# Two blocks of small experts moved to the third and last place, an earlier split of the first token tile, and a gating step moved into the last combination

## The chip, the cores and the metric

The kernel runs on one core of a Trainium2 chip. The metric is device time of one execution in microseconds (us); lower is better. A core has five engines with instruction streams of their own: TensorE (PE: matmuls and transposes; PEld is its weight load), VectorE (DVE), ScalarE (ACT), GpSimd (POOL) and SyncE (SP), which here issues the DMA transfers. They meet through semaphores.

## What is computed

Two layers over x of 512 tokens and 1024 channels, in f32:

```python
h = rms_norm(x, norm_mix)                  # all RMS norms over the 1024 channels
x = x + mixer(h)                           # dilated attention and conformer convolution, gated, w_out
h2 = rms_norm(x, norm_ffn)
# top-1 of 4 groups, then top-2 of 8 experts in it: 2 of 32 experts for each token
x = x + sum_e gate_e * (silu(h2 @ w_gate[e]) * (h2 @ w_up[e])) @ w_down[e]     # FF = 512
x = x + sigmoid(rms_norm(x, norm_ple) @ w_ple_gate) * (p @ w_ple_proj)
```

and a last RMS norm behind the second layer. Every token picks its own experts, so which experts have few tokens is known only at run time.

## The kernel before, in words

**Tiles.** x lies in 4 tiles of 128 tokens by 1024 channels. Dense weights (`wd`) come as chunks of 128 by 1024 (512 KB), are loaded raw (`s_raw`), scaled for the gating chunks (L234), and split into a high part (`s_hi`, ScalarE, L235) and a low part (`s_lo`, GpSimd L240, or in halves on GpSimd and VectorE). `mm3` (L311) multiplies such pairs with three matmuls, high by high, low by high and high by low; these are the rows of L313 to L315. `token_b` (L350) is 24 of these matmuls for one token tile over four chunks and 512 output columns; `tokens_b` runs it for the 4 tiles.

**Start.** `run` (L436) loads the x tiles and the first chunks in turn. For each tile it computes 1/rms (squares on ScalarE, a chain of tiny VectorE operations), then `prep` (L430) makes the normalised `s_n` on VectorE and appends to `todo` the transposes (`ps_tr`, L420) with their high and low halves `s_hTh` and `s_hTl`. An entry of `todo` is run when something pops it. The recording of this part (line 103 in the profile, where a helper records every operation) goes through a scheduler that places the instructions on each engine. Then comes `mixer` (L492). Its first step is the value projection: `tokens_b` over the chunks v0 to v3, into `ps_tb`; behind it the step with `ps_z` begins. `ahead` says how many chunks are split before they are needed.

**Mixture of experts.** `order_experts` (L935) counts the tokens of each expert and sorts: the first 4 experts are static, of the rest the 8 with the fewest tokens are the small ones. Each expert has a place in a table of slots: 64 for an ordinary one, 32 for a small one; tokens beyond that go through `overflow` (L1289), a loop with a count that is read at run time. A block has 128 slots: two ordinary experts (a pair) or four small ones (a quad). `BLK` lists the 14 blocks of a layer: 2 static pairs, 2 quads, 10 pairs. The weights of an expert are 12 tiles of 512 KB (four each of `wg`, `wu`, `wdn`), in a ring of slots that SyncE fills in the order in which they are used (L253).

The loop of `moe` (L1036) takes two blocks a turn, c = 0 to 6: gate and up of both (`ps_g`, `ps_u`), `hidden` (tanh and two products), down of the two blocks of the turn before (`ps_y`), transposes, the gather for the next turn (`ps_xg`), and the combination of the turn before into x (`ps_c`, L1144, `s_x` added at L1153). The experts of a block write to different rows of one PSUM tile, 64 rows each for a pair and 32 for a quad; TensorE runs these column groups side by side. In turn 2 stands the overflow, in turns 4 and 5 the embeddings' projection (`ps_pe`).

**Tail of a layer.** After the loop come the downs of blocks 12 and 13 and their combination, with a hook `then(t)` after each token tile: transposes of x (`ps_tr`, L1269), the parts `s_gTh` and `s_gTl`, the splits of the gating chunks pg0 to pg7 (a list says how many after which tile), and `first(t - 1)`, the first half of the gating matmuls (`ps_tb`). After all four, 1/rms of each tile (`rh`) is computed. `ple` (L1406) then does `gated(t, 0)` for the four tiles (tanh, product L1417, addition to x L1419), and `tokens_b` over pg4 to pg7 with `gated(t, 1)`, which ends with `prep` for the next layer or the last norm and the output.

## Time and profile before

| | |
|---|---|
| median of 3 runs | 1854.9 us (1853.12 to 1855.19) |
| the profiled execution | 1849.56 us, span 1847.8 us |
| mean granted clock of TensorE in it | 0.987 |
| busy: TensorE, VectorE, ScalarE, GpSimd | 95%, 47%, 29%, 21% of the span |
| chain that ended last | TensorE 62%, DMA 21%, VectorE 8%, issue 5% |
| moved by DMA | 478.66 MB, mean 259 GB/s |

The chain is followed back from the last instruction, at each step to what released it. A wait at one place of it belongs to one stage; the shares of the whole span do not say which stage has which limit. Matmuls overlap, so the step from one to the next is shorter than the duration of one (0.23 us against 0.39 us for 512 columns).

### The profile page before, as it was taken

To read this page: it belongs to the slowest core of one execution; us is meant where nothing else is said; L and a number is where in the kernel's file an instruction comes from. 1 tells how busy PE (TensorE), PEld (TensorE's weight loads), DVE (VectorE), ACT (ScalarE), POOL (GpSimd) and SP (SyncE) were. 2 spreads that over 40 slices of the span, in tenths; PEclk is the share of its full clock that TensorE was granted. 3 is DMA by queue.
4 is the path that set the end of the run, shared out by engine and by line. 5 is a ranking of instruction groups with operands and counts; after the bars stand their busy time and mean duration, and the time that the engine had idled before them with its cause. 6 is when DMAs were issued, how large, how long until landed. Compare 5 with 4: busy or idle time off the path is not lost.

```text
span 1847.8 us, 24216 instructions
## 1 busy us (share of the span) xinstructions
PE 1750.0 (95%) x8324; PEld 1055.2 (57%) x8324; DVE 871.8 (47%) x2131; ACT 544.6 (29%) x1041; POOL 379.6 (21%) x203
## 2 busy tenths in 40 slices
PE   5999999989889999999999999999989899999997
PEld 4776777753143455454877777777432443455356
DVE  5587864374041343223558777535620331443146
ACT  4355443321011012112634545342110110121045
POOL 3445332410200001000444443242002000010021
PEclk9999999999999999999999999999999999999999
DMA  5212126479999999997241112554899899999941
GB/s 224 84 65 68 58 79 232 145 264 384 419 359 404 419 419 419 416 419 300 86 133 58 60 57 69 180 195 139 307 391 419 341 418 419 419 414 419 419 197 46
DMA packets 133616, 478.66 MB, mean 259 GB/s; under 512 B 14832, under 2 KB 15344, under 8 KB 133488
## 3 DMA queue, kind: packets, MB, share of 16 engines
q1 hardware_dynamic: 133488, 477.06, 66.4%
q8 instruction: 68, 1.11, 0.2%
q14 instruction: 60, 0.49, 0.1%
HBM read 474.90 MB, written 2.10 MB: 258 GB/s over the span
## 4 chain that ended last, share of the span: by engine, by line
PE 62%; DMA 21%; DVE 8%; issue 5%; ACT 2%; POOL 1%; SPq 0%; POOLq 0%; DVEq 0%; ACTq 0%
DMA s_w<-wdn 11%; PE ps_g L103 8%; PE ps_xg L103 6%; PE ps_u L103 6%; PE ps_z L314 5%; PE ps_z L313 5%; PE ps_z L315 5%; PE ps_y L103 5%; DMA s_w<-wu 5%; PE ps_c L103 5%; DMA s_w<-wg 3%; PE ps_tb L313 2%; PE ps_tb L314 2%; PE ps_tb L315 2%; PE ps_S L634 2%
## 5 line engine op out<-in xcount | busy, mean ns | idle before, releaser
L240 POOL TENSOR_TENSOR s_lo<-s_raw,s_hi 128x1024 fp32r<-128x1024 f32 x114 | 274.8, 2422 | 838.2 <-ACT s_hi L235 464.5
L103 PE MATMUL ps_u<-s_w,s_xg 128*64 128x512 f32 (+1 forms) x1024 | 239.0, 595 | 12.2 <-DMA s_w<-wu 11.8
L103 PE MATMUL ps_g<-s_w,s_xg 128*64 128x512 f32 (+1 forms) x1024 | 225.0, 606 | 14.3 <-DMA s_w<-wdn 9.4
L103 PE MATMUL ps_y<-s_w,s_hT 128*64 128x512 f32 (+1 forms) x1024 | 222.9, 601 | 10.7 <-DMA s_w<-wdn 10.4
L314 PE MATMUL ps_z<-s_hTl,s_hi 128*128 128x512 f32 x512 | 203.9, 398 | 0.0
L313 PE MATMUL ps_z<-s_hTh,s_hi 128*128 128x512 f32 x512 | 201.4, 393 | 0.0
L315 PE MATMUL ps_z<-s_hTh,s_lo 128*128 128x512 f32 x512 | 199.8, 390 | 0.0
L103 PEld LDWEIGHTS ps_u<-s_w,s_xg 128*64 128x64 f32 (+1 forms) x1024 | 67.6, 130 | 178.0 <-issue 118.0
L103 PEld LDWEIGHTS ps_y<-s_w,s_hT 128*64 128x64 f32 (+1 forms) x1024 | 69.2, 131 | 161.7 <-issue 114.3
L103 PEld LDWEIGHTS ps_g<-s_w,s_xg 128*64 128x64 f32 (+1 forms) x1024 | 65.1, 132 | 162.0 <-issue 129.0
L526 DVE SCALAR_TENSOR_TENSOR s_acc<-ps_z,smt,s_acc 128x511 f32<-128x511 f32 (+27 forms) x210 | 153.7, 732 | 4.2
L235 ACT ACTIVATE s_hi<-s_raw 128x1024 fp32r<-128x1024 f32 x120 | 125.4, 1056 | 8.8 <-PE ps_wo L314 4.0
L1108 DVE SCALAR_TENSOR_TENSOR s_h<-s_h,ps_g 128x512 f32<-128x512 f32 x28 | 19.2, 687 | 212.0 <-ACT s_h L1107 194.5
L1107 ACT ACTIVATE s_h<-ps_g,rs 128x512 f32<-128x512 f32 x28 | 19.2, 687 | 328.9 <-PE ps_g L103 327.4
L1153 DVE TENSOR_TENSOR s_x<-s_x,ps_c 128x512 f32<-128x512 f32 x112 | 75.2, 685 | 77.1 <-PE ps_c L103 46.1
L314 PEld LDWEIGHTS ps_z<-s_hTl,s_hi 128*128 128x128 f32 x512 | 96.3, 188 | 21.4 <-issue 3.0
L313 PEld LDWEIGHTS ps_z<-s_hTh,s_hi 128*128 128x128 f32 x512 | 96.1, 188 | 21.3 <-issue 1.0
L103 PE MATMUL ps_xg<-s_OH,s_xh 128*128 128x256 f32 x412 | 104.3, 293 | 3.7 <-DVE s_lgT L944 3.7
L315 PEld LDWEIGHTS ps_z<-s_hTh,s_lo 128*128 128x128 f32 x512 | 96.3, 188 | 19.0
L1118 ACT ACTIVATE s_hT<-ps_hT 128x512 f32<-128x512 f32 x28 | 15.4, 596 | 298.8 <-PE ps_hT L103 298.8
L103 PE MATMUL ps_xg<-s_OH,s_xl 128*128 128x256 f32 x412 | 103.1, 290 | 0.0
L1109 DVE TENSOR_TENSOR s_h<-s_h,ps_u 128x512 f32<-128x512 f32 x28 | 19.2, 687 | 155.2 <-PE ps_u L103 155.2
(274 smaller groups left out, 2815.4 us busy)
## 6 DMA issues: line engine op xcount, KB each, us to landing
s_w<-wu SPq DMA_DIRECT2D x256, 512.0 KB, 9.9
s_w<-wdn SPq DMA_DIRECT2D x256, 512.0 KB, 9.9
s_w<-wg SPq DMA_DIRECT2D x248, 512.0 KB, 9.9
s_raw<-wd SPq DMA_DIRECT2D x124, 512.0 KB, 3.3
s_w<-wg SPq DMA_DIRECT2D x16, 256.0 KB, 7.6
s_x<-x SPq DMA_DIRECT2D x4, 512.0 KB, 9.7
out<-s_n SPq DMA_DIRECT2D x8, 256.0 KB, 2.0
s_gain<-gains SPq DMA_DIRECT2D x3, 512.0 KB, 5.1
```

What stands on the lines that cost most here:

```text
L103: i = f(*a, **k)
L235: nc.scalar.activation(hi, raw, AF.Copy)
L240: nc.gpsimd.tensor_tensor(lo, raw, hi.bitcast(F32), op=OP.subtract)
L313: mm(out, lh, rh, start=start, stop=False)
L314: mm(out, lh, rl, start=False, stop=False)
L315: mm(out, ll, rh, start=False, stop=stop)
L526: v.scalar_tensor_tensor(o, i, w, o, op0=OP.mult, op1=OP.add)
L634: nc.tensor.matmul(ps[:, off:off + n], qk(0, i * P, (i + 1) * P)[r], qk(1, 0, n)[r], start=True, stop=True)
L1107: act.activation(t, pg, AF.Tanh, scale=rh[p])
L1108: v.scalar_tensor_tensor(t, t, 1.0, pg, op0=OP.add, op1=OP.mult)
L1109: v.tensor_mul(t, t, pu)
L1153: v.tensor_add(xs, xs, ps)
```

## The change

It has three parts.

- **Blocks.** The two quads stood third and fourth; now they stand third and last, with the ten pairs between them. `order_experts` gets another rule for the slots' base.
- **Start.** In `run` the transposes of token tile 0 are popped right behind its own `prep`, and the splits of the value chunks are recorded as 0, then 1 and 2, then 3. The other tiles' transposes are popped in the middle of the value projection's `token_b` by a hook, in layer 0 alone. In that stage `ahead` is 1 instead of 4.
- **Gating.** 1/rms of a tile is computed in the combination's hook, and `first(t)` does `gated(t, 0)` at once. `gated` becomes a method; the body is the same.

```diff
--- before.py
+++ after.py
@@ -28,12 +28,12 @@
 GS = 256
 
 
+
 NST, NSM = 4, 8
 NDY = NE - NST
 LD = 4
-BLK = ([(2 * i, 2 * i + 1) for i in range(NST // 2)]
-       + [tuple(range(NST + 4 * i, NST + 4 * i + 4)) for i in range(NSM // 4)]
-       + [(i, i + 1) for i in range(NST + NSM, NE, 2)])
+BLK = ([(2 * i, 2 * i + 1) for i in range(NST // 2)] + [tuple(range(NST, NST + 4))]
+       + [(i, i + 1) for i in range(NST + NSM, NE, 2)] + [tuple(range(NST + 4, NST + NSM))])
 NB = len(BLK)
 
 
@@ -362,11 +362,11 @@
                 self.done(c)
         return ps
 
-    def tokens_b(self, cs, src, then):
+    def tokens_b(self, cs, src, then, hook=None):
         for c in cs:
             self.take(c)
         for t in range(NT):
-            then(t, self.token_b(cs, src, t))
+            then(t, self.token_b(cs, src, t, hook))
 
 
     def rsqrt(self, y, a, t, steps=3):
@@ -443,7 +443,9 @@
         for t in range(NT):
             if t:
                 nc.sync.dma_start(self.x[t], self.dr["x"][t * P:(t + 1) * P])
-            self.load_chunks(t)
+            if t < 3:
+                self.load_chunks(t)
+        self.load_chunks(3)
         self.small(0)
         self.load_chunks(5)
         self.load_c2()
@@ -456,9 +458,9 @@
         for t in range(NT):
             n = self.s4.get(F32, "n")
             self.prep(t, gain, self.rms(t, n), n)
-            if t in (1, 2):
+            self.split_chunks((0, 2, 3, 3)[t])
+            if t == 0:
                 self.todo.pop(0)()
-            self.split_chunks(t)
         self.nc = nc
         self.s4.free()
         for l in range(self.L):
@@ -493,7 +495,7 @@
         nc = self.nc
         v, act = nc.vector, nc.scalar
         base = l * NCH
-        self.look, self.ahead = LK[0], AH
+        self.look, self.ahead = LK[0], AH if l else 1
         pos = self.pos = {s: base + i for i, s in enumerate(SEQ_CHUNKS)}
         self.lim = pos["wo7"]
         conv, attn, side = [], [], []
@@ -505,10 +507,17 @@
         def value(t, ps):
             act.activation(vt(t), ps, AF.Copy)
             self.ps.free()
-            if self.todo:
+            if l and self.todo:
                 self.todo.pop(0)()
-        self.tokens_b([pos[f"v{i}"] for i in range(4)], self.hT, value)
-
+        halves = []
+
+        def middle():
+            halves.append(0)
+            if not l and len(halves) % KD == KD // 2 and self.todo:
+                self.todo.pop(0)()
+        self.tokens_b([pos[f"v{i}"] for i in range(4)], self.hT, value, middle)
+
+        self.ahead = AH
         if l:
             self.load_c2()
         self.scale_small(l)
@@ -937,6 +946,7 @@
         v = self.nc.vector
         cnt = self.posb[:, 128:160]
         key, rank, small, base, self.cnt, top, rest, bs = (self.lgT[:, 32 * i:32 * i + 32] for i in range(8))
+        bs32 = rest
         bs, ss = bs[:, :8], bs[:, 8:16]
         over = lambda a, n: a.unsqueeze(1).to_broadcast([P, n, 32])
         down = lambda a, n: a.unsqueeze(2).to_broadcast([P, n, 32])
@@ -958,10 +968,12 @@
         v.tensor_reduce(rank, t3, axis=AX.X, op=OP.add)
 
         v.tensor_scalar(small, rank, float(NSM), 32.0, op0=OP.is_lt, op1=OP.mult)
-        v.scalar_tensor_tensor(base, rank, float(NSM - 1), small, op0=OP.subtract, op1=OP.mult)
+
+        v.tensor_scalar(bs32, rank, 4.0, -40.0, op0=OP.is_ge, op1=OP.mult)
+        v.scalar_tensor_tensor(bs32, bs32, -11.0, rank, op0=OP.add, op1=OP.add)
+        v.tensor_mul(base, bs32, small)
         v.scalar_tensor_tensor(base, rank, float(CAP), base, op0=OP.mult, op1=OP.subtract)
-        if CAP * NST != CAP // 2 * NSM:
-            v.tensor_scalar(base, base, float(CAP * NST - CAP // 2 * NSM), None, op0=OP.add)
+        v.tensor_scalar(base, base, -128.0, None, op0=OP.add)
         v.tensor_copy(base[:, :NST], self.cc(C_BASE, NST))
         v.tensor_add(self.cnt, cnt, small)
         self.ps.free()
@@ -1254,10 +1266,8 @@
         self.rh = []
         self.src = [lambda k, a, b, s=s: s[a // P][:, k * P:(k + 1) * P] for s in gT]
         cs = [self.pos[f"pg{i}"] for i in range(4)]
-        self.pg = []
-
         def first(t):
-            self.pg.append(self.token_b(cs, self.src, t))
+            self.gated(t, 0, self.token_b(cs, self.src, t))
 
         def then(t):
             if t == NT - 1:
@@ -1273,17 +1283,16 @@
             split_after(PGS[t + 1])
             self.gT[0].append(hi)
             self.gT[1].append(lo)
+            junk = self.s2.get(F32, "j")
+            r = self.rms(t, junk)
+            self.s2.free()
+            h_ = self.tn(1, f"rh{t}")
+            v.tensor_scalar(h_, r, 0.5, None, op0=OP.mult)
+            self.rh.append(h_)
             if t:
                 first(t - 1)
         combine((NB - 2, NB - 1), then)
         first(NT - 1)
-        for t in range(NT):
-            junk = self.s4.get(F32, "j")
-            r = self.rms(t, junk)
-            self.s4.free()
-            h_ = self.tn(1, f"rh{t}")
-            v.tensor_scalar(h_, r, 0.5, None, op0=OP.mult)
-            self.rh.append(h_)
 
 
     def overflow(self, l):
@@ -1403,6 +1412,16 @@
             self.s4.used, self.s2.used, self.ps.used = was
 
 
+    def gated(self, t, h, ps):
+        nc = self.nc
+        th = self.s2.get(F32, "th")
+        self.last = nc.scalar.activation(th, ps, AF.Tanh, scale=self.rh[t]).ins
+        self.ps.free()
+        nc.vector.scalar_tensor_tensor(th, th, 1.0, self.pp[h](t), op0=OP.add, op1=OP.mult)
+        xs = self.x[t][:, h * T:(h + 1) * T]
+        self.last_v = nc.vector.tensor_add(xs, xs, th).ins
+        self.s2.free()
+
     def ple(self, l):
         nc = self.nc
         v, act = nc.vector, nc.scalar
@@ -1410,17 +1429,7 @@
         self.look, self.ahead = 3, 1
         last = l == self.L - 1
 
-        def gated(t, h, ps):
-            th = self.s2.get(F32, "th")
-            self.last = act.activation(th, ps, AF.Tanh, scale=self.rh[t]).ins
-            self.ps.free()
-            v.scalar_tensor_tensor(th, th, 1.0, self.pp[h](t), op0=OP.add, op1=OP.mult)
-            xs = self.x[t][:, h * T:(h + 1) * T]
-            self.last_v = v.tensor_add(xs, xs, th).ins
-            self.s2.free()
-
-        for t in range(NT):
-            gated(t, 0, self.pg[t])
+        gated = self.gated
         self.pp[0].free()
         gain = self.gain_row(l + 1)
         if not last:
```

The order of instructions, at three places. TensorE's first rows: `ps_tr` are transposes of a normalised token tile (`s_n_108` is tile 0, `s_n_131` and `s_n_149` tile 1), `ps_tb` the value matmuls of tile 0. Before:

```order
L420 MATMUL ps_tr_149<-c_71,s_n_108 128x128 x4
L420 MATMUL ps_tr_158<-c_71,s_n_108 128x128 x4
L420 MATMUL ps_tr_190<-c_71,s_n_131 128x128 x4
L420 MATMUL ps_tr_199<-c_71,s_n_131 128x128 x4
L313 MATMUL ps_tb_260<-s_hi_126,s_hTh_100 128x512
```

After:

```order
L420 MATMUL ps_tr_131<-c_71,s_n_108 128x128 x4
L420 MATMUL ps_tr_140<-c_71,s_n_108 128x128 x4
L313 MATMUL ps_tb_230<-s_hi_126,s_hTh_100 128x512
L314 MATMUL ps_tb_230<-s_lo_127,s_hTh_100 128x512
L315 MATMUL ps_tb_230<-s_hi_126,s_hTl_104 128x512
L313 MATMUL ps_tb_230<-s_hi_126,s_hTh_100 128x512
L314 MATMUL ps_tb_230<-s_lo_127,s_hTh_100 128x512
L315 MATMUL ps_tb_230<-s_hi_126,s_hTl_104 128x512
L313 MATMUL ps_tb_230<-s_hi_167,s_hTh_101 128x512
L314 MATMUL ps_tb_230<-s_lo_168,s_hTh_101 128x512
L315 MATMUL ps_tb_230<-s_hi_167,s_hTl_105 128x512
L313 MATMUL ps_tb_230<-s_hi_167,s_hTh_101 128x512
```

The transposes of tile 1 went from the second place to behind ten value matmuls of tile 0.

TensorE, a little further: `s_lo_196` is the low part of the last value chunk, `ps_tb_230` belongs to tile 0, `ps_tb_274` to tile 1, `s_n_177` is tile 2. After:

```order
L313 MATMUL ps_tb_274<-s_hi_167,s_hTh_101 128x512
L314 MATMUL ps_tb_230<-s_lo_196,s_hTh_103 128x512
L315 MATMUL ps_tb_230<-s_hi_195,s_hTl_107 128x512
L314 MATMUL ps_tb_274<-s_lo_168,s_hTh_101 128x512
L315 MATMUL ps_tb_274<-s_hi_167,s_hTl_105 128x512
L420 MATMUL ps_tr_287<-c_71,s_n_177 128x128 x4
```

The last two matmuls of tile 0 were set behind ten of tile 1.

VectorE in the last combination of layer 0, at its last token tile: `ps_c` is the combination's output, `s_gTl` the low part of the transposed x. Before:

```order
L1153 TENSOR_TENSOR s_x_3972<-s_x_3972,ps_c_6756 128x512
L1153 TENSOR_TENSOR s_x_3972<-s_x_3972,ps_c_6762 128x512
L1271 TENSOR_TENSOR s_gTl_6769<-ps_tr_6770,s_gTh_6768 128x512
L1271 TENSOR_TENSOR s_gTl_6769<-ps_tr_6777,s_gTh_6768 128x512
L393 TENSOR_SCALAR rms_6851<-ss_0_6847 128x1
```

After:

```order
L1165 TENSOR_TENSOR s_x_3902<-s_x_3902,ps_c_6824 128x512
L401 TENSOR_SCALAR rms_6781<-rms_6781 128x1
L1420 SCALAR_TENSOR_TENSOR s_th_6820<-s_th_6820,s_pp_5678 128x512
L402 TENSOR_SCALAR rms_6781<-rms_6781 128x1
L1422 TENSOR_TENSOR s_x_3900<-s_x_3900,s_th_6820 128x512
L1290 TENSOR_SCALAR rh_6793<-rms_6781 128x1
L1165 TENSOR_TENSOR s_x_3902<-s_x_3902,ps_c_6830 128x512
L1281 TENSOR_TENSOR s_gTl_6837<-ps_tr_6838,s_gTh_6836 128x512
```

Between the two additions of the last tile now stand steps of the 1/rms of tile 2, and the product (L1420) and addition (L1422) of tile 1's gating.

## Rows read from the trace of the kernel before

**Rows 1.** The page's slices of the span (40 equal slices of 46.2 us; busy tenths of TensorE, and what the DMA engines moved).

```profile
PE   5999999989889999999999999999989899999997
...
GB/s 224 84 65 68 58 79 232 145 264 384 419 359 404 419 419 419 416 419 300 86 133 58 60 57 69 180 195 139 307 391 419 341 418 419 419 414 419 419 197 46
```

**Rows 2.** SyncE's queue in time, and the page's list of DMA issues. Columns of the first four: start us, us from the first to the last issue, queue and line, what is loaded, how many tiles. The last row: size of one, median us from issue to landing.

```profile
798.00 9.08 SPq L253 DMA_DIRECT2D s_w<-wu  x8
...
808.00 39.58 SPq L253 DMA_DIRECT2D s_w<-wdn  x32
...
848.45 9.06 SPq L217 DMA_DIRECT2D s_raw<-wd  x8
...
1719.63 39.63 SPq L253 DMA_DIRECT2D s_w<-wdn  x32
...
s_w<-wdn SPq DMA_DIRECT2D x256, 512.0 KB, 9.9
```

**Rows 3.** The chain of waits, in order of time: start us, us, what (engine, tile written, line, how many). Layer 0 but for the last row, which is layer 1.

```profile
504.32 13.88 PE ps_y L103 x64
...
801.37 7.02 PE ps_g L103 x32
...
816.76 10.44 DMA s_w<-wdn
...
847.17 8.48 PE ps_c L103 x29
...
855.64 13.94 PE ps_y L103 x64
...
1765.03 13.93 PE ps_y L103 x64
```

**Rows 4.** TensorE's timeline in the first block of small experts (start us, us, line, tiles, matmuls in a row, in brackets the idle time before and what ended it), then a window: us, busy us (instructions) of PE, PEld, DVE, ACT, POOL, granted clock, DMA share, GB/s.

```profile
436.74 7.07 PE L103 MATMUL ps_g<-s_w,s_xg 128*32 128x512 f32 x64
...
446.82 2.25 PE L103 MATMUL ps_u<-s_w,s_xg 128*32 128x512 f32 x12 [1.29 <-DMA s_w<-wu]
...
452.49 2.26 PE L103 MATMUL ps_u<-s_w,s_xg 128*32 128x512 f32 x12 [0.18 <-DMA s_w<-wu]
...
450.00:475.00 25.00, 21.64 (x81) 3.90 (x80) 0.69 (x1) 0.00 (x0) 0.00 (x0) 1.00 1.03 419
```

**Rows 5.** A row of SyncE's queue, two windows (columns as above) and one row of TensorE's waits from 385 to 870 (line waited for: us in total, times, longest).

```profile
523.67 13.40 SPq L253 DMA_DIRECT2D s_w<-wu  x8
...
550.00:552.00 2.00, 0.00 (x0) 0.00 (x0) 0.00 (x0) 0.00 (x0) 0.00 (x0) 0.72 0.21 82
...
552.00:556.00 4.00, 3.20 (x8) 1.01 (x10) 0.06 (x1) 0.00 (x0) 0.00 (x0) 0.50 0.49 131
...
PE ps_g L103 <- DMA s_w<-wdn: 4.7, 1, 4.7
```

**Rows 6.** The timeline of the start on VectorE, TensorE and GpSimd, in order of time, and one window (columns as above).

```profile
15.34 2.13 DVE L103 SCALAR_TENSOR_TENSOR s_n<-s_x,rms,s_gain 128x1024 f32<-128x1024 f32 x1
...
17.62 1.94 PE L420 MATMUL ps_tr<-c,s_n 128*128 128x128 f32 x8 [5.26 <-DVE s_n L103]
...
19.21 0.78 PE L313 MATMUL ps_tb<-s_hi,s_hTh 128*128 128x512 f32 x1
...
19.82 2.02 DVE L103 TENSOR_SCALAR rms<-rms 128x1 int32<-128x1 int32 x9
...
20.64 0.63 PE L313 MATMUL ps_tb<-s_hi,s_hTh 128*128 128x512 f32 x1
...
21.07 0.63 PE L314 MATMUL ps_tb<-s_lo,s_hTh 128*128 128x512 f32 x1
...
26.23 8.04 POOL L240 TENSOR_TENSOR s_lo<-s_raw,s_hi 128x1024 fp32r<-128x1024 f32 x3 [1.34 <-ACT s_hi L235]
...
29.29 2.77 DVE L103 SCALAR_TENSOR_TENSOR s_n<-s_x,rms,s_gain 128x1024 f32<-128x1024 f32 x1
...
31.99 2.83 DVE L103 TENSOR_TENSOR s_lo<-s_raw,s_hi 128x512 fp32r<-128x512 f32 x1
...
34.87 0.50 PE L314 MATMUL ps_tb<-s_lo,s_hTh 128*128 128x512 f32 x1 [2.25 <-DVE s_lo L103]
...
37.00:39.00 2.00, 2.00 (x8) 1.71 (x7) 1.30 (x4) 1.81 (x5) 0.00 (x0) 0.52 0.28 109
...
48.85 0.39 PE L315 MATMUL ps_tb<-s_hi,s_hTl 128*128 128x512 f32 x1
...
49.08 0.39 PE L313 MATMUL ps_z<-s_hTh,s_hi 128*128 128x512 f32 x1
```

**Rows 7.** The end of layer 0: TensorE's waits from 862 to 1000, then the timeline of VectorE and GpSimd, then the matmuls of `ps_z` from 900 to 1000 (duration ns min/median/max, first and last start).

```profile
PE ps_tr L1269 <- DVE s_x L1153: 3.0, 3, 2.5
...
PE ps_tr L420 <- DVE s_n L432: 2.5, 2, 2.2
...
908.63 0.68 DVE L1417 SCALAR_TENSOR_TENSOR s_th<-s_th,s_pp 128x512 f32<-128x512 f32 x1
...
912.69 2.83 DVE L1417 SCALAR_TENSOR_TENSOR s_th<-s_th,s_pp 128x512 f32<-128x512 f32 x1
...
912.41 2.56 POOL L240 TENSOR_TENSOR s_lo<-s_raw,s_hi 128x1024 fp32r<-128x1024 f32 x1 [6.46 <-ACT s_hi L235]
...
L313 PE MATMUL ps_z<-s_hTh,s_hi x55: 387/389/397, 959.4 to 999.5; 128*128 128x512 f32 x55
```

## The prediction, made before the change was run

> **What bounds the kernel now.** I read the slices of the span first [rows 1]. TensorE's row is full except in the first slice, and the transfer row reaches its ceiling of 419 GB/s in two long stretches only, the two mixtures of experts (MoE). So the mixers are bound by TensorE, and inside the MoE two engines of about equal load share the lead: a pair of experts is 24 weight tiles, a quad of small ones 48, at 1.25 us a tile (eight tiles are issued in 9.08 us, seven steps [rows 2]), thus 30 and 60 us of transfer. TensorE needs the same time for either, because the column groups of a block run at once: 7.0 us for the 32 matmuls of a pair's gate group, 7.1 us for the 64 of a quad's [rows 3, 4]. A pair is balanced between the two, a quad is bound by its transfer.
>
> The chain of waits then says what ends each MoE [rows 3]. In layer 0 it runs over transfers from 816.76 on (10.44 us is the first of three such pieces), then a combination, and then 13.94 us of `ps_y` matmuls to 869.6 without a wait for a transfer. The last weight tile was issued at 808.00 + 39.58 = 847.6 and landed 9.9 us later, at 857.5 [rows 2]. TensorE thus ends 12.1 us behind the last byte. In layer 1 the same sum is 1719.63 + 39.63 + 9.9 = 1769.2 against 1765.03 + 13.93 = 1779.0, 9.8 us. This is the work of a pair that TensorE still has in hand when its transfer has ended.
>
> **Order of the blocks.** The bytes and their number stay. What moves is the transfer-bound block: 24 tiles (30 us) go from the fourth place to the last. TensorE, which reaches the downs of blocks 0 and 1 at 504.3 in layer 0 [rows 3], would no longer wait for a second quad before them, so it is about 20 us early there and, with the 8 down tiles less that follow, 30 us early after the next downs; the stream's order shifts by the same 24 tiles, and the pairs between see the same relation of slots and consumers. In the last two blocks the stream gets its 24 tiles back, while TensorE needs no more time, so it falls back to the transfer: down of blocks 10 and 11 is fed while landing, their combination and down of block 12 lie beside the last 24 tiles (30 us, against 8.48 us for 29 of 32 matmuls and half of 13.94), and down of block 13 eats its tiles as they land. After the last byte is left one quarter of a down (four steps over FF), 6.97/4 = 1.7 us. End of the MoE: 857.5 + 1.7 = 859.2 instead of 869.6, **−10.4 us** in layer 0, and 1770.9 instead of 1779.0, **−8.1 us** in layer 1. I count −10 and −8. The eight gating chunks are queued behind the last weights [rows 2]; 1.25 us apart they land from 858.8, and the first two are all that the next step on ScalarE asks for.
>
> The bounds: nothing at all, if the stream is held up by 10 us more than before, and −12 with −10 if the stream even closes one of its gaps. It has such gaps [rows 5]: where the up-weights of a block wait for slots (13.40 us for eight tiles instead of 9.08, 4.3 us) and around the overflow loop (82 GB/s from 550 to 552, while TensorE stood 4.7 us). Both stand at the same turn of the loop after the change, some 20 to 30 us earlier, and their instructions and slots are the same; I take them as unchanged.
>
> The longer rule for the slots' base is three more operations over 32 columns on VectorE, in a chain whose like last 0.22 us each (2.02 us for nine [rows 6]). They stand before the first transfer of a chosen expert, with the static blocks' tiles still in the queue as cover; I count nothing, and +1 per layer without that cover.
>
> **Start.** The PE rows of the start [rows 6] show the transposes of token tile 0 done at 12.36, idle 5.26 us until the normalised tile 1 (VectorE, 15.34 + 2.13), the first value matmul at 19.21, a stall before 34.87 (its last 2.25 us behind the low half of a split; that and `s_n` of tile 3 take 2.83 and 2.77 us on VectorE beside three GpSimd splits from 26.23), and the first `ps_z` at 49.08. From 19.21 there is 96 × 0.227 = 21.8 us of matmuls at full step, so 8 us go elsewhere: the stall, the transposes of tiles 2 and 3, and matmuls at a step of 0.43 us after each idle time (20.64 to 21.07, against 0.23 from 48.85 to 49.08; after the stall the granted clock was 0.52 from 37 to 39).
>
> In the new order tile 0's matmuls stand ahead of tile 1's transposes, so six can run from about 13.5 on. What bounds next is VectorE: `s_n` of tile 1 ends at about 18.3 (0.8 later, since ScalarE's halves of tile 0 go ahead of tile 1's squares), then two low halves, the chain of tile 2's 1/rms (2.02 us for its nine steps, some 2.5 in all) and its `s_n` (up to 2.1), and the low half of the last value chunk, at about 25. TensorE has parked only two matmuls for that, and from there 60 matmuls (13.6 us) and 16 transposes (2.1) are left with the following inputs ready: first `ps_z` at 41 to 42 if no wait and no low clock remains, 45 to 47 with low steps twice. I take 44, **−5 us** (bounds −2 and −7.5): the three long splits on GpSimd that slowed VectorE are moved behind the value stage, which favours the early end. It is TensorE's time in a mixer bound by TensorE, so it stays.
>
> **1/rms and half of the gating within the combination.** Between the end of down in layer 0 and layer 1's first `ps_z` lie 959.4 − 869.6 = 89.8 us [rows 3, 7], of which TensorE waits 3.0 us for `s_x` and 2.5 us for `s_n`. The 2.5 is `s_n` behind a crowd on VectorE from 903 on: four 1/rms chains and the gating of all tiles follow one another, one product in 2.83 us where another took 0.68. The change spreads them over the four tokens of the combination, where TensorE has some 8 us of work for each (24 gating and 8 combination matmuls at 0.23, and transposes). The wait of 2.5 should go. Against it stand ScalarE's two squares per token ahead of `s_gTh`, and the last token's second `s_x` addition, which is now queued behind tile 1's tanh and its gating product; I price that at +1.2 us, the tanh plus the product less the slack of one matmul group. I take **−2.5 us** at the boundary with the low clock that follows the waits, and **+0.5** at the end of layer 1, where no `s_n` is waited for. Bounds: −5 and +4 per layer. What follows the last matmul is not touched.
>
> A row first: the gating product takes 2.83 us from 912.69 and the same operation 0.68 from 908.63; a GpSimd split runs from 912.41 to 914.97 [rows 7]. The Trainium skill, "SBUF — State Buffer", section "SBUF: two separate sides", says that a VectorE instruction with two SBUF operands and a GpSimd instruction that reads SBUF lock each other out of a shared port for the whole instruction. The trace agrees, and by that rule the moved products and additions would be as slow wherever a gating chunk is split beside them, which is what the combination's stretch is full of.
>
> **Sum.** −10 − 8 − 5 − 2.5 + 0.5 = −25 us. The profiled execution took 1849.56 us, 5.3 below the median, so it would be 1824.6; against the median of 1854.9 it gives **1830 us**.
>
> **Rivals.**
> *The stream pays it back.* If the gaps of [rows 5] grow by 10 us, because TensorE is no longer starved after the third block and the transfer meets full slots more often, the last byte lands later and the order of the blocks gains nothing: −7 us, **1848**. For it: pairs are balanced to within a microsecond or two, so each pause of TensorE can reach the stream. Against it: both chains of waits lie on transfers up to the last downs. 11 in 100.
> *VectorE becomes the bound of the combination.* Per token: four tile operations (2.8 us), the chain (2.5), product and addition, 1.4 alone and 5.6 if each meets a split: 6.7 to 10.9 us against TensorE's 8. At the upper end 3 us for each of three tokens, half of it in both layers +9: **1839**. 10 in 100.
> *The clock falls at the end of the MoE* (the slower side). TensorE would wait on transfers from about 785 (the pair before the last, 30 us earlier than now) to 828 (857.5 less 24 tiles). If the granted clock drops there to 1.2 GHz and stays for what follows, that runs at 0.43 instead of 0.227 a matmul: 26 us for the downs of 10 and 11, 19 for their combination, 26 for the last two downs, from 809 to 880: 10 us later than now in place of 10 earlier, +20 on the forecast in each layer, **1870**. It decides from a loss of some 12 us a layer on. For it: 0.50 was granted from 552 to 556, after 4.7 us of waiting [rows 5]. Against it: with two quads in a row the same pattern of short waits (0.2 to 1.3 us) runs from 450 on at 1.00 [rows 4]. 4 in 100.
> The Trainium skill, "TensorE: Matmul & The Clock Gate", section "HAM oscillation — how this bites in real kernels", describes a kernel whose work per tile is shorter than the wait for the next tile's transfer and whose clock falls again in each wait, so that each tile starts cold. By that rule this rival would be the likely one; the quads of this trace do not agree with it.
>
> **How the numbers follow.** Forecast 71 (1820 to 1838), VectorE 10 (1836 to 1843), stream 11 (1843 to 1850), clock 4, and 4 for more gain than counted (start at 41, gaps closed: 1812 to 1820). A range of 1817 to 1844 leaves out some 15. What a measurement here can tell from no change is about 0.2%, 3.7 us: faster by more 0.93, within 0.03, slower 0.04.
>
> **What would show it.** In the new trace: the last weight tile should be issued at about the same distance from the first gate matmul as now, with `ps_y` ending 2 us after its landing and the chain of waits on `s_w<-wdn` to the end; TensorE's waits for weights in the last block of 0.2 to 1.3 us at clock 1.00; first `ps_z` at 42 to 47; no wait for `s_n` L432 at the boundary. I am wrong if the gaps between weight issues add up to 10 us more per layer, if the clock of the last block is below 1.00, or if TensorE waits for `s_x` or `s_gTh` by over 4 us in a combination.

## The result and the profile after

| | before | after |
|---|---|---|
| median | 1854.01 us (4 runs, 1853.11 to 1855.19) | 1825.74 us (4 runs, 1824.82 to 1827.75) |
| the profiled execution | 1849.56 us, span 1847.8 us | 1824.82 us, span 1823.0 us |

The ratio is 0.9849 (95% interval 0.9832 to 0.9866): 28.3 us less, 1.5%. The forecast was 25 us less and 1830 us. The two traces are only 24.7 us apart; why the medians are further apart comes with the second trace of the kernel before, below.

The first view is the slices of the changed kernel's span, to be read against [rows 1]: both long stretches of the transfer stay near 419 as before, the first now with 403 instead of 300 in its last slice, and TensorE's row is at 8 or 9 tenths between the first slice and the last, as before.

```profile
PE   6999999989999999999999999999999999999897
...
PEclk9999999999999999999999999999999999999998
...
GB/s 244 76 59 70 58 79 228 155 240 394 419 347 419 419 419 409 419 419 403 60 134 70 59 58 70 173 196 147 309 390 392 380 418 419 419 410 419 419 238 47
```

The second is SyncE's queue at the end of both mixtures of experts (start us, us to the last issue, line, what, how many), which answers to [rows 2]. Now 40 down tiles close each one instead of 32, and the last is issued at 844.4 and at 1740.2.

```profile
795.07 49.32 SPq L253 DMA_DIRECT2D s_w<-wdn  x40
...
845.27 9.05 SPq L217 DMA_DIRECT2D s_raw<-wd  x8
...
1689.82 50.33 SPq L253 DMA_DIRECT2D s_w<-wdn  x40
```

The third is the chain of waits there (start us, us, what), which answers to [rows 3]. It lies on transfers to 853.9, and behind the last one stand ten `ps_y` matmuls in 1.9 us, where 64 of them took 13.94 us.

```profile
834.08 9.87 DMA s_w<-wdn
...
844.06 9.87 DMA s_w<-wdn
...
853.97 1.90 PE ps_y L103 x10
855.88 2.16 PE ps_c L1162 x8
```

Stage by stage, from TensorE's timeline (each stage from the first matmul of one kind to that of the next, in us). The last two columns are the ranges over the other traces of this study that have the old part, or the new one, in that stage (variants of a part left out); there were fourteen traces.

| stage | before | after | unchanged part in other traces | changed part in other traces |
|---|---|---|---|---|
| start to the first `ps_z` | 49.08 | 44.38 | 47.72 to 49.69 | 43.68 to 45.49 (same start) |
| mixer and routing, layer 0 | 348.4 | 350.1 | 347.7 to 351.1 | |
| first gate matmul to the last `ps_y`, layer 0 | 471.47 | 460.83 | 471.25 to 471.55 | 460.25 to 461.73 (quads third and last) |
| from there to the first `ps_z` of layer 1 | 90.48 | 86.10 | 88.77 to 90.43 | 86.08 to 88.96 (new gating) |
| mixer and routing, layer 1 | 349.5 | 349.3 | 348.1 to 351.0 | |
| first gate matmul to the last `ps_y`, layer 1 | 469.42 | 460.36 | 468.93 to 472.09 | 461.01 to 462.44 |
| from there to the last matmul | 59.36 | 61.91 | 60.65 to 60.99 | 60.16 to 63.22 |

### The profile page after: what moved, and what is told of

Read it like the earlier page. It is cut to its first block, busy times and chain, and to the rows that moved or that the text cites. A ratio compares the mean times of both kernels' runs of the same rounds, so it can differ in the third digit from the quotient of the medians.

```text
span 1823.0 us, 24216 instructions
## 1 busy us (share of the span) xinstructions
PE 1737.6 (95%) x8324; PEld 1053.0 (58%) x8324; DVE 880.4 (48%) x2137; ACT 544.8 (30%) x1041; POOL 378.3 (21%) x203
## 4 chain that ended last, share of the span: by engine, by line
PE 63%; DMA 22%; DVE 7%; issue 5%; POOL 1%; ACT 1%; SPq 0%; DVEq 0%; POOLq 0%; ACTq 0%
DMA s_w<-wdn 11%; PE ps_g L103 8%; DMA s_w<-wu 7%; PE ps_z L313 6%; PE ps_z L314 6%; PE ps_z L315 6%; PE ps_u L103 5%; PE ps_xg L103 5%; PE ps_y L103 5%; PE ps_c L103 4%; DMA s_w<-wg 3%; PE ps_tb L313 3%; PE ps_tb L315 3%; PE ps_tb L314 3%; PE ps_S L643 2%
## 5 line engine op out<-in xcount | busy, mean ns | idle before, releaser
L103 PE MATMUL ps_y<-s_w,s_hT 128*64 128x512 f32 (+1 forms) x1024 | 227.6, 601 | 10.2 <-DMA s_w<-wdn 9.4
L103 PE MATMUL ps_g<-s_w,s_xg 128*64 128x512 f32 (+1 forms) x1024 | 207.6, 605 | 8.7 <-DMA s_w<-wdn 7.6
L1120 DVE SCALAR_TENSOR_TENSOR s_h<-s_h,ps_g 128x512 f32<-128x512 f32 x28 | 19.2, 687 | 189.7 <-ACT s_h L1119 183.3
L1119 ACT ACTIVATE s_h<-ps_g,rs 128x512 f32<-128x512 f32 x28 | 19.2, 687 | 306.6 <-PE ps_g L103 305.0
L313 PEld LDWEIGHTS ps_z<-s_hTh,s_hi 128*128 128x128 f32 x512 | 96.5, 188 | 21.4 <-issue 1.0
L315 PEld LDWEIGHTS ps_z<-s_hTh,s_lo 128*128 128x128 f32 x512 | 96.6, 189 | 19.1
```

The costliest lines, as they stand in the source:

```text
L103: i = f(*a, **k)
L313: mm(out, lh, rh, start=start, stop=False)
L315: mm(out, ll, rh, start=False, stop=stop)
L1119: act.activation(t, pg, AF.Tanh, scale=rh[p])
L1120: v.scalar_tensor_tensor(t, t, 1.0, pg, op0=OP.add, op1=OP.mult)
```

## The experiments

Each time stands beside that of the kernel before, timed in turn with it on the same chip. Line numbers in their rows can be a few off those of the changed kernel. Of longer edits only the part that matters is shown, and a line with `BLK` gives the order in words.

### Each part alone

**Blocks.** The new `BLK` and the rule for the base in the kernel before:

```diff
-BLK = (static pairs + quads + pairs)
+BLK = (static pairs + quad + pairs + quad)
```

> Only the order of the blocks and the rule for the slots' base are changed. Theory (a quad in the last place lets TensorE end right behind the last weight, in both layers): 18 us below the kernel before, 16 to 20; each layer's last down ends 9 to 10 us earlier, nothing else moves. Rival (the three parts need each other: the order pays only because the gating no longer stands behind it): 10 us or less.

Measured: 1832.08 us against 1854.33, ratio 0.9884 (0.9869 to 0.9899), 22 us. In its trace the two mixtures of experts take 460.25 and 462.44 us, 11.1 and 8.1 us less than the means with the old order. That is 19.2 us. The other 3 us, by which the time falls below the expected range, are not in these stages. The blocks need neither of the other parts.

**Start.** The loading, the splits, `ahead` and the hook of the start in the kernel before:

```diff
+            self.split_chunks((0, 2, 3, 3)[t])
+            if t == 0:
                 self.todo.pop(0)()
...
-        self.look, self.ahead = LK[0], AH
+        self.look, self.ahead = LK[0], AH if l else 1
```

> Only the start is changed. In the changed kernel the value stage ended 4.7 us earlier, but the first gate matmul of layer 0 came only 3.0 us earlier: behind the same wait of 1.0 us for s_S in the mixer the granted clock fell to 0.50 there and not in the kernel before. Theory (the clock's answer to a short wait goes with the place in time, so it repeats with this start): first ps_z 4.7 us earlier, 2.8 to 3.0 us at the end. Rival (a single event of that execution): 4.7 us at the end, clock 1.00 behind that wait.

Measured: 1848.62 us, ratio 0.9973 (0.9962 to 0.9983), 5.7 us. First `ps_z` at 43.81. In its mixer the clock stayed at 1.00 behind the wait for `s_S`, and the first gate matmul came 4.1 us earlier than in the first trace of before. So the fall in the changed kernel's trace does not go with this start, as the rival had it. It was not unique either: behind the same wait the clock fell to 0.50 in three of the fourteen traces, two with the new start (the changed kernel and `q_both_last2`, further down) and one with the old (`a_only`).

**Gating.** 1/rms and `gated(t, 0)` within the combination, in the kernel before:

```diff
-            self.pg.append(self.token_b(cs, self.src, t))
+            self.gated(t, 0, self.token_b(cs, self.src, t))
```

> Only 1/rms and the gating are moved. Theory (as predicted in sign; sizes from the changed kernel's trace: 4.4 us less between layer 0's last down and layer 1's first ps_z, 2.5 us more in layer 1's tail): 1 to 3 us below the kernel before. Rival (the tail of layer 0 gained because the pg chunks arrive later beside it, thus from the order of the blocks): no gain, 0 to +3 us.

Measured: 1848.27 us, ratio 0.9973 (0.9962 to 0.9983), 6.1 us, twice the upper end of what was expected. In its trace the tail of layer 0 is 1.5 us shorter and that of layer 1 1.1 us longer than in the first trace of before. With the time lost to a low clock taken off each (the length of the stage times what the granted clock lacks to 1: 1.7 us of the old tail of layer 0 and 3.4 of the new one), they are 3.2 us shorter and 1.1 us longer. That is 2.1 us, within what was expected. The rival falls, since with the blocks alone the tail of layer 0 is 88.8 us by this reckoning, as before. The other 4 us are not in the tails: against the second trace of before (further down), which is near that kernel's median, the start is 2.0 us shorter and the second mixture of experts 3.2, stages that this edit does not touch. One trace can't tell whether that recurs, and it stays open. The three parts alone add up to 34 us, against 28.3 together; the four intervals leave some 5 us to either side of that difference, so it may be chance, but gains that overlap are not ruled out.

### Gating in layer 0 alone

```diff
         def first(t):
...
+            if l == self.L - 1:
+                self.pg.append(self.token_b(cs, self.src, t))
+            else:
                 self.gated(t, 0, self.token_b(cs, self.src, t))
```

> The changed kernel, but in layer 1 1/rms and the first half of the gating stand behind the last combination again, as before. Theory (in layer 1 nothing is waited for that the move could spare, and the last tile's second addition to x stands behind the gating): 2 to 2.5 us below the changed kernel, about 1823 us. Rival (layer 1's tail lost to the clock, not to the move): within 1 us of the changed kernel.

Measured: 1825.43 us, ratio 0.9842 (0.9828 to 0.9856). That is the changed kernel's time, so the rival holds: most of the 2.5 us that layer 1's tail was longer in the changed kernel's trace were the clock's. Tails of layer 1 in which the clock stays up before the last matmul take 59.36 us with the old gating (before) and 60.16 to 60.41 with the new one (five traces): the move costs 1 us there.

### The kernel before, once more

> The kernel before once more, unchanged, for a second trace. In the traces so far the granted clock falls in episodes that each cost 1.7 or 3.4 us of work, and their number before the last matmul differs from one execution to the next. The first trace of before was 3.6 us faster than its slowest relative among the plain runs' lowest and 4.8 below their median. Theory (episodes of the clock make the difference): the stages without an episode agree within 0.5 us with the first trace, and the rest of any difference in span is a multiple of about 1.7. Rival (another stage was shorter then): a stage without an episode differs by over 1 us.

Measured: 1854.88 us, span 1853.1, 5.3 us more than the first trace. The first mixture of experts agrees within 0.1 us (471.47 and 471.55); the start and the first mixer with its routing take 0.6 and 0.75 us more. The second mixture of experts takes 2.7 us more and the last tail 1.5 us more. The tail has an episode of low clock that the first trace lacks. In the second mixture of experts both traces lose 5.1 us to a low clock, but one episode stands at another place: from 1558 in the first trace, in the midst of the stream, and from 1760 in the second, where TensorE works off what it has in hand at the end. Of the 2.7 us, 1.1 are in the stream itself and 1.6 behind its last issue. Windows of the second trace (us, busy us and instructions of PE, PEld, DVE, ACT, POOL, granted clock, DMA share, GB/s):

```profile
1758.00:1760.00 2.00, 1.21 (x3) 0.56 (x3) 1.52 (x3) 2.00 (x4) 0.00 (x0) 1.00 1.03 420
1760.00:1762.00 2.00, 1.55 (x4) 1.16 (x4) 1.77 (x3) 0.18 (x1) 0.00 (x0) 0.54 1.02 418
1762.00:1764.00 2.00, 2.00 (x7) 1.57 (x6) 0.81 (x2) 0.00 (x0) 0.00 (x0) 0.61 1.03 420
```

The same place of the first trace:

```profile
1755.00:1757.00 2.00, 0.66 (x2) 0.35 (x2) 0.96 (x2) 2.00 (x4) 0.00 (x0) 1.00 1.02 416
1757.00:1759.00 2.00, 1.56 (x6) 0.93 (x7) 2.00 (x4) 0.74 (x2) 0.00 (x0) 1.00 1.03 420
1759.00:1761.00 2.00, 2.00 (x10) 1.65 (x9) 1.53 (x3) 0.00 (x0) 0.00 (x0) 1.00 1.03 422
```

Both show TensorE waiting for `s_yl` and then at work. In the one the clock falls to half, in the other it does not. The theory holds for some 3 of the 5.3 us. The start's 0.6 and the stream's 1.1 are not the clock's, so the rival has a part in it too. The prediction's base of 1849.56 lay 5.3 us below that kernel's median in part because its episodes stood where they cost less.

### Where the second quad stands

The rule for the base gets other constants, and where a pair stands behind the quad, one more step that moves its slots:

```diff
-BLK = static pairs + [quad] + 10 pairs + [quad]
+BLK = static pairs + [quad] + 9 pairs + [quad] + 1 pair      # q12
+BLK = static pairs + [quad] + 8 pairs + [quad] + 2 pairs     # q11
+BLK = static pairs + 10 pairs + [quad] + [quad]              # q_both_last, q_both_last2
```

> The changed kernel with the second block of small experts in the place before the last; a pair stands last. Theory (what counts is that TensorE, starved by the quad, comes to the last downs with no work in hand): the last down still ends 1.7 us behind the last byte, thus within 2 us of the changed kernel, about 1826. Rival (the quad must be last, since a pair leaves its own work behind the last byte as before): a layer's last down ends 8 to 12 us behind the last byte, 1840 or more.

Measured: 1826.06 us, ratio 0.9856 (0.9842 to 0.9871), the changed kernel's time.

> The changed kernel with the second block of small experts two places before the last. Theory (by the order of tiles: downs 10 and 11 end with their 24 tiles 20 us before the last byte, then 10 us of transposes and combination, then two downs of 7 us): the last down ends about 6 us behind the last byte, 4 us later than in the changed kernel in each layer, about 1834. Rival (starved is starved: the lead is kept over two blocks): within 2 us of the changed kernel. Rival 2 (the quad must be last): 1845 or more.

Measured: 1839.29 us, ratio 0.9926 (0.9913 to 0.994), 13.5 us above the changed kernel; 8 were expected. The down tiles at the end of layer 0 in SyncE's queue:

```profile
794.23 49.59 SPq L252 DMA_DIRECT2D s_w<-wdn  x40
```

and a window of the combination before the last downs (columns as above):

```profile
840.00:845.00 5.00, 5.00 (x17) 3.98 (x18) 3.10 (x5) 0.00 (x0) 0.00 (x0) 0.75 1.02 419
```

The last tile is issued at 843.8, as early as in the changed kernel, and the last `ps_y` starts 17.4 us later instead of 10.9 (17.1 in layer 1). Of the 6.5 us, some 1.7 are the clock's (0.75 in that window), which leaves the 4 to 5 that the order of the tiles gives.

> The changed kernel with both blocks of small experts in the last two places, and 9 instead of 3 slots kept free in the last turn, which these blocks need. Theory (the stream sets the end, and the pairs from the third block on still leave TensorE a little faster than the stream): last down 1.7 us behind the last byte as in the changed kernel, within 2 us of it. Rival (with pairs from the third block on TensorE is not starved early, so the stream meets full slots and loses time): the last byte lands 5 to 15 us later per layer, 1835 to 1855.

Measured: 1846.63 us, ratio 0.9963 (0.995 to 0.9977). This is the rival's time, but not for its reason. SyncE's queue at the end of layer 0:

```profile
782.79 52.08 SPq L252 DMA_DIRECT2D s_w<-wdn  x42
...
835.75 9.06 SPq L216 DMA_DIRECT2D s_raw<-wd  x8
...
845.80 6.55 SPq L252 DMA_DIRECT2D s_w<-wdn  x6
```

and TensorE's waits from 800 to 880 (line waited for: us in total, times, longest):

```profile
PE ps_y L102 <- DMA s_w<-wdn: 12.1, 11, 10.2
```

The 42nd tile was issued at 834.9. The missing six, had they come next, would have been out at 842.4, which is 450.0 us behind that trace's first gate matmul, as in every other order. They stood behind the eight gating chunks, since with nine slots kept free the last six found no place in time, and TensorE waited 10.2 us. The next kernel keeps three slots free again and also loads the gating chunks later; which of the two would do alone was not run. The second edit:

```diff
-        self.load_chunks(self.lim)
         down(NB - 2)
+        self.load_chunks(self.lim)
         down(NB - 1)
```

> The changed kernel with both blocks of small experts in the last two places, 3 free slots in the last turn as in the changed kernel, and the loading of the gating chunks written behind the down of block 12, so that all 48 last down tiles stand ahead of the gating chunks in the queue. In the earlier version of this order 6 down tiles stood behind the 8 gating chunks, and TensorE waited 10.2 us for them. Theory (it was this queue order alone; the stream lost nothing in the pairs before): within 2 us of the changed kernel, about 1826, last down about 2 us behind the last byte. Rival (with quads last the slots are too few and the stream stalls at the end whatever the order): 1835 or more.

Measured: 1826.43 us, ratio 0.9858 (0.984 to 0.9876): the changed kernel's time again, and this row of its queue:

```profile
784.32 59.57 SPq L252 DMA_DIRECT2D s_w<-wdn  x48
```

The five orders in one table, without the queue order of the first `q_both_last`. First column: from the first gate matmul to the last issue of a weight tile (the stream); second: from that issue to the start of the last `ps_y` (10 us of it the transfer itself); layer 0 and layer 1, in us.

| second quad | stream | TensorE behind it | time |
|---|---|---|---|
| fourth place (before) | 450.1, 450.4 | 21.4, 19.1 | 1854.0 |
| twelfth (q11) | 450.0, 450.7 | 17.4, 17.1 | 1839.3 |
| thirteenth (q12) | 450.1, 450.3 | 10.6, 10.9 | 1826.1 |
| last (the change) | 449.9, 449.5 | 10.9, 10.9 | 1825.7 |
| last, and the first quad thirteenth | 450.1, 450.9 | 10.9, 10.8 | 1826.4 |

### The stream as the bound

```diff
-                if p == 2 * OVC:
-                    self.overflow(l)
```

> The changed kernel without the loop for tokens beyond an expert's places, so those tokens' shares are left out; everything else stays. Around the loop the transfer stream loses about 4 us in each layer (the windows from 526 to 534 of the changed kernel). Theory (the end of the MoE is the end of the stream): both gaps go to the end, 7 to 10 us below the changed kernel, 1816 to 1819. Rival (the stream has slack at that place and catches up through full slots): within 3 us of the changed kernel.

Measured: 1817.52 us, ratio 0.9797 (0.9784 to 0.981), 8.2 us below the changed kernel. Its last weights are issued 4.0 and 1.7 us earlier, counted from the first gate matmul, and its two mixtures of experts are shorter by as much. That is 5.7 of the 8.2 us. The rest is in other stages: in the mixer of layer 0 and in the last tail the changed kernel's trace loses 1.7 us each to a low clock that this one does not. Windows of the changed kernel around the loop (columns as above):

```profile
526.00:528.00 2.00, 0.00 (x0) 0.00 (x0) 0.00 (x0) 0.00 (x0) 0.00 (x0) 1.00 0.46 184
528.00:530.00 2.00, 1.43 (x6) 0.54 (x8) 0.06 (x1) 0.00 (x0) 0.00 (x0) 0.78 0.21 55
```

and of the kernel without it:

```profile
526.00:528.00 2.00, 2.00 (x12) 0.72 (x10) 0.00 (x0) 0.00 (x0) 0.00 (x0) 1.00 1.02 416
528.00:530.00 2.00, 2.00 (x12) 0.68 (x10) 0.00 (x0) 0.00 (x0) 0.00 (x0) 1.00 1.02 418
```

In both layers the last `ps_y` starts as long behind the last issue as in the changed kernel (10.9 us), so the gap taken out of the stream comes off the end.

### The splits beside the value projection

```diff
-        self.look, self.ahead = LK[0], AH if l else 1
+        self.look, self.ahead = LK[0], AH
```

> The changed kernel, but chunks are again split four ahead during the value projection, so GpSimd's long splits stand beside VectorE's work at the start. Theory (the early transposes carry the gain, and the long splits beside s_n and the low halves cost 2 us each, partly on the path): first ps_z at 45 to 47 instead of 44.4. Rival (the long splits were the whole loss of the start): first ps_z at 48 or later, the gain of the start gone. Rival 2: no matter, 44 to 45.

Measured: 1828.79 us, ratio 0.9866 (0.9851 to 0.9881), 3 us above the changed kernel; first `ps_z` at 47.93. TensorE, GpSimd and VectorE in the timeline of that start:

```profile
28.60 0.50 PE L314 MATMUL ps_tb<-s_lo,s_hTh 128*128 128x512 f32 x1 [1.98 <-DVE s_lo L103]
...
22.30 5.70 POOL L240 TENSOR_TENSOR s_lo<-s_raw,s_hi 128x1024 fp32r<-128x1024 f32 x2 [1.49 <-ACT s_hi L235]
...
25.72 2.83 DVE L103 TENSOR_TENSOR s_lo<-s_raw,s_hi 128x512 fp32r<-128x512 f32 x1
```

and in the changed kernel:

```profile
27.96 0.50 PE L314 MATMUL ps_tb<-s_lo,s_hTh 128*128 128x512 f32 x1 [0.27 <-DVE s_lo L103]
...
23.74 2.40 POOL L240 TENSOR_TENSOR s_lo<-s_raw,s_hi 128x1024 fp32r<-128x1024 f32 x1 [3.88 <-ACT s_hi L235]
...
23.88 3.34 DVE L103 SCALAR_TENSOR_TENSOR s_n<-s_x,rms,s_gain 128x1024 f32<-128x1024 f32 x1
27.14 0.77 DVE L103 TENSOR_TENSOR s_lo<-s_raw,s_hi 128x512 fp32r<-128x512 f32 x1
...
31.13 1.27 DVE L103 SCALAR_TENSOR_TENSOR s_n<-s_x,rms,s_gain 128x1024 f32<-128x1024 f32 x1
...
44.38 0.39 PE L313 MATMUL ps_z<-s_hTh,s_hi 128*128 128x512 f32 x1
```

The theory is wrong here. With the early transposes but the old lead of the splits, 3.5 of the 4.3 us (means, below) are gone: unless GpSimd's long splits are taken away from VectorE's operations, the rest of the new start brings under 1 us. What the shorter lead would bring with the old order of transposes was not run. It also moves ScalarE's copies (`s_hi`), but the wait of 1.98 us is for VectorE's `s_lo`.

### The gating one tile later

```diff
         def first(t):
-            self.gated(t, 0, self.token_b(cs, self.src, t))
+            held.append((t, self.token_b(cs, self.src, t)))
+            if len(held) > 1:
+                u, ps = held.pop(0)
+                self.gated(u, 0, ps)
```

(the last one is done behind `first(NT - 1)`).

> The changed kernel, but the gating of a tile is done one tile later, so that on VectorE the last tile's two additions to x follow each other again. In the changed kernel TensorE waits 2.8 us for s_x in each layer's last combination, most of it at the last tile. Theory (this wait is the queueing behind the gating that was priced at 1.2 us): s_x waits below 1.5 us per layer, 1 to 3 us below the changed kernel in each tail, about 1822. Rival (s_x waits for the combination's matmuls and ScalarE anyway): waits as now, within 1 us.

Measured: 1822.68 us, ratio 0.983 (0.9816 to 0.9843). It is the lowest time of a kernel that does all the work, 3.1 us below the changed kernel by the medians; the two intervals overlap. TensorE's waits from 840 to 1000 in the changed kernel:

```profile
PE ps_tr L1279 <- DVE s_x L1165: 2.8, 3, 1.5
PE ps_tb L315 <- DVE s_gTl L1281: 0.8, 1, 0.8
```

and from 840 to 960 in this one:

```profile
PE ps_tr L1284 <- DVE rh L1295: 1.6, 1, 1.6
PE ps_tb L315 <- DVE s_gTl L1286: 0.8, 1, 0.8
...
PE ps_tr L1284 <- DVE s_x L1165: 0.3, 1, 0.3
```

The wait for `s_x` is gone but for 0.3 us, and over half of it came back under another name. The rows around it, in this kernel:

```profile
877.39 2.70 DVE L1429 TENSOR_TENSOR s_x<-s_x,s_th 128x512 f32<-128x512 f32 x1
...
880.14 0.67 DVE L1165 TENSOR_TENSOR s_x<-s_x,ps_c 128x512 f32<-128x512 f32 x1
...
876.62 2.92 POOL L240 TENSOR_TENSOR s_lo<-s_raw,s_hi 128x1024 fp32r<-128x1024 f32 x1 [1.92 <-ACT s_hi L235]
...
880.87 1.60 PE L1284 MATMUL ps_tr<-c,s_x 128*128 128x128 f32 x8 [1.64 <-DVE rh L1295]
```

The profile names `rh`, a step of 0.14 us, but the transposes wait for the last tile's first addition (880.14). That stands on VectorE behind the addition of a tile's gating, which takes 2.70 us from 877.39 beside a GpSimd split; in the changed kernel the same addition took 0.68 us without one (at 881.29). About 1 us is saved in each tail by the waits; the rest of the 3.1 us may be the clock's.

## Why the prediction was right, step by step

**Order of the blocks: −18 forecast, −19.6 in the stages.** Over the traces with either order the means are 471.4 and 460.9 us in layer 0 and 470.5 and 461.4 in layer 1, thus −10.5 and −9.1 against −10 and −8. The mechanism is shown by three things that could have come out otherwise. The stream from the first gate matmul to the last tile has the same length in all five orders, to 1.4 us, and two traces of the kernel before differ by as much (450.1 and 451.2 in layer 0, 450.4 and 451.5 in layer 1). What changes is TensorE's work behind it, and it follows the place of the quad as the tiles' order says. A gap taken out of the stream comes off the end. The rival in which the stream pays it back falls: the gaps of [rows 5] stand at the same turn, some 25 us earlier.

The quad need not be last. In the place before the last it does the same; what counts is that TensorE comes to the last downs with no work in hand. The prediction tied it to the last place and didn't see that.

**Start: −5 forecast, −4.3 measured** (means of 48.7 and 44.4 over the traces with either start). The step that failed is which part carries it: the text let VectorE's chain behind tile 0 set the new end and took the moved splits as something that "favours the early end". Without them under 1 us of the gain is left. The chain itself ended at 27.9 instead of about 25, in part because `s_n` of tile 2 took 3.34 us where up to 2.1 were counted. That the sum came out is luck, since both were in it. Of the 4.7 us in the changed kernel's trace only 3.0 reached the first gate matmul; that loss was an episode of the clock in the mixer, which seven of the nine traces with this start lack.

**Gating: −2.5 and +0.5 forecast.** At the boundary the wait for `s_n` is gone (no such row among the waits above, 2.4 us still with the blocks alone), and the means of the stage are 90.0 and 86.8 us. Of the 4.4 us between the two traces 1.7 are an episode of low clock in the old tail. With the time lost to a low clock taken off, the stage is 88.7 to 88.8 us in all four traces with the old gating and 85.6 to 86.2 in the nine with the new: −2.7, near the forecast. In layer 1 the same reckoning gives 59.0 to 59.4 and 59.8 to 60.4 us, +1.0. The waits that make this up are not those of the forecast, which priced the last tile's addition at 1.2 us. First the rows of the kernel before, the second tile and the last, then both halves of the last tile in the changed kernel:

```profile
877.95 0.65 PE L1269 MATMUL ps_tr<-c,s_x 128*128 128x128 f32 x4 [2.52 <-DVE s_x L1153]
...
897.02 0.65 PE L1269 MATMUL ps_tr<-c,s_x 128*128 128x128 f32 x4 [0.25 <-DVE s_x L1153]
```

```profile
880.52 0.66 PE L1279 MATMUL ps_tr<-c,s_x 128*128 128x128 f32 x4 [1.06 <-DVE s_x L1165]
...
882.69 0.66 PE L1279 MATMUL ps_tr<-c,s_x 128*128 128x128 f32 x4 [1.51 <-DVE s_x L1165]
```

The last tile waits 2.3 us more, about twice the price, and the 2.5 us at the second tile are gone, which the forecast did not look at: TensorE waits 2.8 us for `s_x` and 0.8 for `s_gTl`, against 3.0 for `s_x` before. So the small cost came out by two errors that nearly cancel.

**VectorE as the bound** did not come, though it is close, and ScalarE with it. Over the first 40 us of the stage they are busy 30.70 and 30.76 us (from 855), in the kernel before 18.23 and 28.83 (from 868). A window of the new combination shows both busy for most of it, 21.45 and 22.36 of 25 us (columns as above):

```profile
855.00:880.00 25.00, 23.30 (x110) 17.11 (x104) 21.45 (x53) 22.36 (x40) 11.34 (x6) 1.00 0.55 208
```

**The clock at the end of the MoE** did not fall for long. Windows of the last two blocks, in which TensorE waits for many of the tiles:

```profile
780.00:805.00 25.00, 23.17 (x133) 5.13 (x130) 1.38 (x2) 0.69 (x1) 0.00 (x0) 1.00 1.03 419
805.00:830.00 25.00, 21.80 (x77) 6.95 (x75) 2.35 (x4) 3.36 (x6) 0.00 (x0) 0.99 1.03 419
830.00:855.00 25.00, 24.44 (x125) 11.07 (x125) 8.06 (x12) 1.41 (x3) 0.00 (x0) 0.94 1.02 419
```

Through the waits for tiles, up to 829, it is 1.00. The one dip (from 829 on) comes behind the wait of the combination for `s_yh`. It is a sign of being wrong that the prediction named, a clock below 1.00 in the last block, but the transfer hides it: in the traces of `a_only` and `c_layer0`, which lack this dip, the last `ps_y` starts as long behind the last issue, 10.9 us. The Trainium skill, "TensorE: Matmul & The Clock Gate", section "HAM oscillation — how this bites in real kernels", tells of a kernel whose waits for a tile are longer than its work on one, and which falls cold in each. Here the waits for tiles are 0.2 to 0.6 us (0.9 at most in layer 1) behind 1 to 5 us of work, so the prediction went too far in calling the clock's fall likely by that rule, and this trace shows no fall in them. In `q_both_last`, where TensorE waited 10.2 us for a tile, the clock was 0.50 from 848 to 861, and that agrees.

**The sum.** By the means of the traces the stages give −10.5 − 9.1 − 4.3 − 3.2 + 0.5 = −26.6; the medians −28.3, and the interval of the ratio −25 to −31. Against the forecast the blocks brought 1.6 us more, the boundary with its clock 0.7 more, and the start 0.7 less; the remaining 1.7 us are in no stage and within the interval. That the base lay below the median was passed over in the prediction by shifting the sum up to it; it was right to do so, though it gave no reason.

## What to carry to other kernels

Where two engines are balanced over blocks of different kinds, a block that is bound by the transfer stream belongs at the end of the stream, or one place before it: it lets the consumer run out of work there, and the end of the stage is the end of the transfer. Measure it by two lengths, the stream and what the consumer still has in hand behind its last byte; the first doesn't change with the order, the second does. Take work of GpSimd on SBUF away from a stretch in which VectorE's operations are on the path; the late gating still waits for one of them. And look at two traces of a kernel before a difference of 2 us between stages is explained.

## What the runs showed of the hardware

The granted clock falls in single episodes, and the same wait is followed by one in one execution and by none in another. Two windows of the changed kernel's mixer (columns as above):

```profile
181.00:183.00 2.00, 2.00 (x7) 1.52 (x6) 0.47 (x3) 2.00 (x9) 2.00 (x2) 0.50 0.00 0
183.00:185.00 2.00, 2.00 (x7) 1.58 (x6) 0.71 (x2) 0.22 (x1) 1.88 (x2) 0.66 0.00 0
```

behind this wait (from 175 to 200):

```profile
PE ps_PT L677 <- DVE s_S L665: 1.0, 1, 1.0
```

The same place in the kernel before, window and wait (from 180 to 205):

```profile
186.00:188.00 2.00, 2.00 (x10) 1.63 (x9) 1.12 (x3) 1.84 (x7) 1.92 (x3) 1.00 0.00 0
```

```profile
PE ps_PT L668 <- DVE s_S L656: 1.0, 1, 1.0
```

TensorE works through both windows of the first at half clock for part of them, and loses 2 × 0.50 + 2 × 0.34 = 1.7 us of full-clock time. This loss, or twice it, is that of nearly all episodes before the last matmul in the fourteen traces, six to ten in each. It is a part of why executions of one kernel scatter by 2 to 5 us, but the mean clock does not order their times: the kernel before took 1850.61 and 1855.27 us at the same 0.987. Where an episode stands counts too, as the dip at 829 and the kernel's second trace show. A stage of one trace can't be told from the same stage of another by less than 1.7 us unless the clock is read with it.

The second is that VectorE's operation of 128 x 1024 on two SBUF operands took 3.34 us beside a GpSimd split and 1.27 us without one (the `s_n` of two tiles, at 23.88 and 31.13 in the changed kernel, the split at 23.74). The Trainium skill, "SBUF — State Buffer", section "SBUF: two separate sides", gives a lock on a shared port for such pairs, and this trace agrees.
